# Another emission order for an attention kernel with bias: the same instructions, written in another sequence

## The chip, the cores and the metric

The kernel runs on one core of one Trainium2 chip. The metric is device time in microseconds, the median of repeated runs. Before the change it is 224.82 us (three runs, 223.55 to 225.61). The profiled execution took 223.97 us.

## The reference

Softmax attention over 4 batches times 8 heads, 1024 queries and keys, 64 channels, with one additive bias shared by all heads:

```python
scores = scale * np.matmul(q, k.transpose(0, 1, 3, 2))   # scale = 1/8
scores = scores + bias                                    # (1, 1, 1024, 1024)
attn = np.exp(scores - max) / (sum(np.exp(scores - max)) + 1e-8)
return np.matmul(attn, v)
```

q, k, v are float32 of shape (4, 8, 1024, 64). The kernel leaves the subtraction of the maximum out, since the inputs are small, and carries the bias as described below.

## The kernel before, in words

**Slots.** Each of 32 heads has 8 chunks of 128 queries, so there are 256 units of work, called slots. For each slot TensorE (PE) makes 1024 keys x 128 queries of scores in PSUM: two halves, tokens `F` and `G` (line 376, tile `pl`), each of four 128-column matmuls, or of two 256-column ones where two neighbouring chunks of a head share a round. `pl` has three double banks, so at most three slots are in flight. Only the first head of a run adds the bias with extra matmuls (line 373); the later ones carry the difference in an enlarged contraction: 64 rows hold this head's q and k, the other 64 hold the negated q and the k of the head before, and so PSUM is never cleared and each fill moves the bank from one head's scores to the next one's. A bank must have been read before it is filled again.

**Exponentials.** For 227 slots ScalarE (ACT) reads the banks and writes the exponential to `E` (line 399): tokens `X`, and `P`/`Q` where a round of three slots is read in two steps of three half banks. For 29 slots VectorE (DVE) makes it in six steps, tokens `f r s h c l` (scale to an integer in `dy`, which frees the bank, then fraction, square, shift, cube, and a last step that assembles the result in `de`).

**Output.** Token `A` multiplies a slot's exponentials with v (line 462, eight matmuls of 65 columns into `po`; the 65th column sums the row). Up to seven slots share a PSUM bank of `po`. There are two such banks, `xa` and `xb`; the letter behind an `A` opens a new one. The transposes of q and k (token `T`, lines 276 and 282, tile `px`) use the same two. `R` takes the reciprocals of a full bank and `M` multiplies and writes `ob` (both DVE), and `M` issues the stores: slots of one bank that are neighbours in head and chunk are joined into one store (line 664, SP's queue).

**Preparation of a pair of heads.** Loads go through GpSimd's (POOL's) queue: k, q at lines 213, 222 and 233, v at 246 and 250, bias at 239. `S` (DVE) sets two heads side by side, `T` transposes, `C` copies out of PSUM, `D` (DVE) makes the negated or shifted copies for the first nine pairs. From pair 9 on, `N` negates q on DVE and DMAs in SP's queue (line 603) place `ke` and `qe`. `V` (DVE) places the v rows of early pairs.

**What sets the order.** Nothing is scheduled by rules: the string `ORDER` lists 1430 tokens, and each engine gets its instructions in the order of that list. The tokens `U` and `L` each issue the next load of a fixed list; `L` also makes it wait for the DVE instruction last written before it. `SIZES` says how many slots each of 38 output banks takes. An engine runs its own list strictly in order; between engines semaphores wait for data and buffers. A load also waits for the landing of one issued four or five places before it.

```python
for token in ORDER.split():
    do(token)
...
asked.append(vec.last if kind == "L" else None)
...
flight.append(jobs.pop(0)().ins)
j = i - (BEHIND[i] if i < len(BEHIND) else 4)
```

Of the kernel before, what the change touches and what calls it, by code (L numbers as in the profile page):

```python
# [8 lines left out]
F32 = mybir.dt.float32  # L9
# [18 lines left out]
F50 G50 Tr0b r43 X50 A38 F51 Cr0 G51 F52 X51 A39 Dr0p3 Dq6p2 F53 G53 r48 A37 X53 G52 F54 R5 r32 G54 X52 Sr1 F56 s43
G56 X54 Dr0p1 F55 s32 Tr1b X56 M5 G55 F57 G57 X55 Cr1 F59 G59 h43 A42a Dr1p0 A56 X57 Dr1p1 F58 h32 G58 f59 A46 X58 A44
F60 G60 A45 c32 X60 F61 G61 s48 A47 F62 X61 A54b R6 L U r59 G62 F63 A49 L M6 X62 F64 G64 l32 A50 X64 L U U A55 G63  # L30
A53a h48 A62 X63 F65 R7 c43 G65 F67 L G67 M7 X65 A61 c48 A51 A52 F66 s59 X67 G66 F68 G68 A60 X66 f68 F70 G70 A58 A63b
X70 F69 l43 G69 F71 A57 X69 G71 F73 r68 l48 A67 X71 F72 G72 A66 G73 X72 F74 R8 h59 G74 X73 F75 f74 L G75 A65 X75 A48
F76 G76 M8 A64 X76 F77 R9 G77 s68 A73a F78 X77 G78 c59 L F79 G79 A69 l59 L U X79 A70 F80 G80 A76 X78 f80 F82 G82 A72
A75 X82 F81 M9 G81 F83 r74 G83 X81 F85 G85 f83 A43 A71b X85 F84 G84 A81 r83 X84 F86 G86 A78 Dq8p1 L U F88 X86 s74 G88
F87 G87 s83 A82 X87 A79 h74 L F89 G89 h68 L U A77 X88 A59 F90 R11 R10 c74 G90 X89 F91 M10 G91 X90 l74 F92 X91 G92 M11
A32a F93 r80 X92 G93 A87 A91 s80 F94 X93 G94 A85 h83 F95 c68 G95 X94 A92 A74 A84 F96 X95 h80 G96 A89b R12 c83 F97 M12
G97 X96 F98 c80 A90 G98 X97 A86 l68 A88 F99 G99 X98 Tq9a A94 Cq9 F100 X99 G100 A93 l80 A68 F101 X100 G101 F102 Tk9a
R13 X101 M13 G102 F103 Nq9 L G103 A96b X102 Ck9 L F104 G104 A101 f104 A97 X103 F105 G105 Tk10a X105 l83 F106 G106 F107
G107 X106 F108 f107 G108 A80 A100 X108 F109 G109 Ck10 A99 X109 F110 G110 r107 A95 F111 X110 R14 G111 M14 A98a F112
A106 r104 X111 G112 Tq10b A103 X112 Cq10 F113 G113 A109 F114 Nq10 X113 G114 s107 Tq11b F115 X114 Cq11 G115 F116 G116  # L40
h107 L A108 X115 F117 f116 L U G117 Tk12b X117 F118 G118 Ck12 A105 A102 X118 F120 R15 G120 s104 Tk11b X120 F121 M15
G121 F119 Ck11 L G119 X121 F123 G123 f119 A83a A112 X123 F124 G124 Tq12b c107 X124 F122 Cq12 G122 F126 A110 X122 l107
L G126 A114 F127 X126 G127 A113 r119 F125 A111 X127 G125 s119 Tk13b F129 h104 X125 G129 Ck13 A115 F130 G130 R16 X129
Nq11 L U A118b F128 Nq12 A124 c104 G128 X130 A117 A123 h119 L F132 r116 G132 A130 X128 A121 A120 l104 X132 F131 G131
F133 M16 L G133 X131 F135 G135 f135 L A126a X133 F134 G134 A122 X134 A127 R17 L s116 F138 G138 F136 M17 X138 G136 F137
G137 f136 Tk14b X137 F141 G141 A129 Ck14 X141 F139 G139 c119 F140 G140 Tq14b X139 h116 r135 A104 F144 X140 Cq14 L F142
G142 A125 r136 G144 X142 A128 A137b R18 L U U F143 s136 X144 G143 F145 c116 L U G145 A107 X145 A133 s135 F147 A132 M18
G147 X143 A131 F148 l116 A138 G148 X147 F146 A134 G146 R19 Tq13a X148 M19 F150 G150 h135 A141b X146 h136 F151 G151
Cq13 L U U A139 A116 X150 c136 F149 G149 A140 l119 X151 F153 Tq15a X149 F154 G154 G153 A142 Nq13 Cq15 X154 F152 Nq15
G152 A143 f152 A119 X153 F157 G157 A147a X157 c135 F156 G156 F155 G155 X156 F160 f155 G160 A145 A144 X160 F159 G159  # L50
R20 A146 Nq14 X159 F158 r155 G158 A149 F163 r152 L U U X158 F162 G163 M20 A151 G162 X163 s155 A148 F161 R21 A153b M21
X162 F166 G166 l135 A156 A150 X166 G161 Tk15a h155 L F165 X161 Ck15 G165 F169 G169 c155 A159 X165 A161 F164 G164 X169
# [652 lines left out]
```

## Time and profile before

| | |
|---|---|
| median of three runs | 224.82 us (223.55 to 225.61) |
| profiled execution | 223.97 us, its span 222.2 us |
| PE busy | 214.5 us |
| ACT busy | 211.6 us |
| DVE busy | 203.6 us |
| POOL (DMA issues) busy | 72.0 us |
| granted TensorE clock | full in all 40 slices |

Three engines are busy for over nine tenths of the span. Busy time says little here: instructions of one engine overlap, and a PE that waits between matmuls is still mostly shown busy. What is read below is start-to-start spacing, what ended an engine's idle time, and the chain of work that ended last. In a row of the timeline come the start, the time from the first start to the last end, the engine, the line, the instruction with its tiles (out<-in), the count, and in brackets idle time of the engine ahead of it with what ended it.

### The profile page before, as it was taken

Reading aid. Unit: us, or ns where it says so; the run is one execution under the profiler, and the core shown is the slowest. Engines: PE = TensorE matmul, PEld = TensorE weight load, DVE = VectorE, ACT = ScalarE, POOL = GpSimd, SP = SyncE. Lnnn points to the kernel's source line nnn. Section 1 sums busy time; section 2 is a strip of 40 time slices with the busy share of each in tenths; the row PEclk is TensorE's granted clock in tenths of the full one; section 3 lists DMA queues with packets and bytes.
Section 4 is the critical chain, followed back from the end, with each engine's and each line's share of the span. In section 5 each row is a group of like instructions: output and inputs, shape, how many; then the busy total and the mean of one; then the engine's idle time right before and its main releaser. Section 6 shows DMA issues by size and latency. Waiting matters only on the chain.

```text
span 222.2 us, 9043 instructions
## 1 busy us (share of the span) xinstructions
PE 214.5 (97%) x3965; PEld 197.5 (89%) x3965; DVE 203.6 (92%) x354; ACT 211.6 (95%) x229; POOL 72.0 (32%) x90
## 2 busy tenths in 40 slices
PE   7799999999999999999999999999999999999993
PEld 2689999999999999999998998898988999899992
DVE  2679999999999999999999999989998999999993
ACT  2799999999999999999999999999999999999992
POOL 8824446637464563030635675410000000000000
PEclk9999999999999999999999999999999999999999
DMA  6999999999999999297899999992111112011213
GB/s 174 227 205 216 227 236 146 173 168 190 128 169 164 88 119 166 62 91 176 102 227 204 215 144 190 119 194 57 44 43 33 55 45 66 7 44 44 86 46 106
DMA packets 86327, 28.87 MB, mean 130 GB/s; under 512 B 66384, under 2 KB 83024, under 8 KB 86288
## 3 DMA queue, kind: packets, MB, share of 16 engines
q0 software_dynamic: 62880, 14.06, 69.9%
q1 hardware_dynamic: 22704, 13.44, 22.6%
q10 hardware_dynamic: 704, 0.79, 1.3%
q8 instruction: 31, 0.51, 1.0%
q14 instruction: 8, 0.07, 0.1%
HBM read 29.36 MB, written 8.39 MB: 170 GB/s over the span
## 4 chain that ended last, share of the span: by engine, by line
ACT 78%; PE 17%; DMA 2%; DVE 1%; issue 0%; SPq 0%; DVEq 0%
ACT E L399 78%; PE pl L376 9%; PE po L462 4%; DMA dy<-in_k_dram 2%; PE px L276 2%; PE pl L373 1%; PE px L282 0%; DVE ob L85 0%; DVE de L85 0%; SPq L501 0%; DVE ko L85 0%; PE pl L276 0%; DVE rs L85 0%; DVEq L85 0%
## 5 line engine op out<-in xcount | busy, mean ns | idle before, releaser
L399 ACT ACTIVATE E<-pl 128x1024 bf16<-128x1024 f32 (+2 forms) x225 | 208.7, 1110 | 1.7 <-PE pl L376 1.6
L462 PE MATMUL po<-vall,E 128*128 128x65 bf16 x1816 | 86.9, 194 | 0.4 <-DVE ob L85 0.2
L462 PEld LDWEIGHTS <-E 128*128 128x128 bf16 x1816 | 77.3, 98 | 3.0 <-DVE ob L85 0.4
L376 PE MATMUL pl<-qo,ko 128*128 128x128 bf16 (+1 forms) x752 | 77.9, 239 | 0.6
L376 PE MATMUL pl<-qe,ke 128*128 128x128 bf16 (+1 forms) x648 | 67.2, 239 | 0.5 <-DVE qe L85 0.2
L376 PEld LDWEIGHTS <-ko 128*128 128x128 bf16 x856 | 57.4, 98 | 6.0 <-ACT E L399 2.1
L376 PEld LDWEIGHTS <-ke 128*128 128x128 bf16 x648 | 43.4, 98 | 5.1 <-ACT E L399 2.2
L85 DVE TENSOR_SCALAR dy<-pl 128x1024 int32<-128x1024 f32 x29 | 35.4, 1221 | 3.7 <-PE pl L376 3.4
L85 DVE SCALAR_TENSOR_TENSOR de<-dy,ds 128x1024 uint16<-128x1024 int32 x29 | 35.1, 1217 | 0.2
L213 POOL DMA_DIRECT2D q<-in_q_dram x18 | 16.6, 921 | 23.8 <-DVE de L85 8.8
L213 POOL DMA_DIRECT2D k<-in_k_dram x18 | 15.9, 887 | 24.1 <-DVE q L85 10.2
L85 DVE TENSOR_TENSOR ob<-po,rs 128x448 f32<-128x448 f32 (+3 forms) x38 | 22.7, 600 | 0.4
L250 POOL DMA_DIRECT2D vall<-in_v_dram x18 | 17.9, 996 | 11.9 <-DVE de L85 4.2
L85 DVE TENSOR_SCALAR de<-dy 128x1024 f16<-128x1024 uint16 x29 | 19.8, 695 | 0.1
L85 DVE TENSOR_TENSOR ds<-de 128x1024 f16<-128x1024 f16 x29 | 19.5, 674 | 0.2
L85 DVE TENSOR_TENSOR ds<-ds,de 128x1024 f16<-128x1024 f16 x29 | 19.5, 679 | 0.0
L373 PE MATMUL pl<-ident,braw 128*128 128x128 bf16 x136 | 14.0, 227 | 0.0
L85 DVE TENSOR_SCALAR qo<-px,sgn 128x1024 bf16<-128x1024 bf16 (+2 forms) x18 | 12.3, 684 | 0.7 <-PE px L276 0.7
L85 DVE TENSOR_SCALAR de<-de 128x1024 f16<-128x1024 f16 x29 | 12.6, 444 | 0.1
L462 PE MATMUL po<-vall,de 128*128 128x65 bf16 x232 | 12.5, 194 | 0.0
L373 PEld LDWEIGHTS <-braw 128*128 128x128 bf16 x136 | 11.8, 148 | 0.4
L85 DVE COPY ko<-px 128x1024 bf16<-128x1024 bf16 (+1 forms) x16 | 10.7, 669 | 1.0 <-PE px L282 1.0
(54 smaller groups left out, 126.0 us busy)
## 6 DMA issues: line engine op xcount, KB each, us to landing
ke<-ko SPq DMA_DIRECT2D x20, 128.0 KB, 4.7
k<-in_k_dram POOLq DMA_DIRECT2D x18, 128.0 KB, 5.3
q<-in_q_dram POOLq DMA_DIRECT2D x18, 128.0 KB, 4.8
out_dram<-ob SPq DMA_DIRECT2D x24, 96.0 KB, 2.8
vall<-in_v_dram POOLq DMA_DIRECT2D x18, 128.0 KB, 6.0
out_dram<-ob SPq DMA_DIRECT2D x30, 64.0 KB, 2.2
braw<-in_bias_dram POOLq DMA_DIRECT2D x7, 256.0 KB, 6.2
de<-in_v_dram POOLq DMA_DIRECT2D x7, 256.0 KB, 7.5
```

What stands on the lines that cost most here:

```text
L85: i = getattr(self.engine, name)(*args, **kwargs)
L213: return nc.gpsimd.dma_start(out=t[:, :, y, :], in_=(qf, kf)[x][pr][:, y].rearrange("p (c d) -> p c d", d=D))
L250: return nc.gpsimd.dma_start(out=vall[:, (2 * pr + t) % VR, :, :D], in_=vf[pr][:, t])
L276: m = nc.tensor.transpose(px[:, c, :], raws[pr, which, c0][:, c].rearrange("p t d -> p (t d)"), ident[:])
L373: m = nc.tensor.matmul(to, braw[:, c1, :].rearrange("p (kp kc) -> p kc kp", kc=NCH)[:, kc, :], ident8[:], start=i == 0 and order[0] == "b" ...
L376: m = nc.tensor.matmul(pl[:, 2 * x + b, i * P:(i + n) * P], kk[:, kc, :], qq[:, c:c + n, :].rearrange("p c q -> p (c q)"), start=i == 0 an ...
L399: read(nc.scalar.activation(E[:, e0:e0 + n].rearrange("p b x -> p (b x)"), pl[:, b0:b0 + n].rearrange("p b x -> p (b x)"), ACTF.Exp, scale ...
L462: nc.tensor.matmul(bank[b][:, banks[b].index(s), :], weights(s, kc), vall[:, slots[s][2] % VR, kc, :], start=first and kc == 0, stop=kc == ...
```

## The change

Only `ORDER` and `SIZES` change. The 1430 tokens are the same ones, but for the letters that choose between `xa` and `xb`, which of the load tokens stand where, and which `A` opens a bank. The same 29 slots go to DVE; the list of loads is the same. Which slots share an output bank changes, and with it the number of stores: 116 before, 162 now, of the same bytes. The part of a store that is contiguous in DRAM is 64, 128 or 192 floats for one row; counted as such pieces, 7,040 of 256 bytes, 6,528 of 512 and 4,224 of 768 become 17,152, 4,736 and 2,048. One pair's transpose (`Tr0`) now stands ahead of the step that sets its heads side by side (`Sr0`), so it takes ten small transposes in place of five; the step itself is still done, 38 exponentials later, and nothing reads it.

```diff
-U U U U U U U U U U U U U U U U U U U U U U U U U U U U U U U U U F3 G3 Tk1a X3 F4 Ck1 G4 F2 Tq1b X4 Dk1p0 G2 Cq1
+L F3 G3 Tk1a F4 Ck1 G4 L Dk1p0 F2 U U Tq1b X3 G2 Cq1 Dq1p0 X4 F6 Dq1p1 G6 Dk1p1 U U X2 U U Sk2 F5 U L G5 F7 Tk2a L Sq2
...
-G29 A18 F30 R2 Dk6p0 G30 X29 F31 M2 Tq6b V4 G31 X30 F32 Cq6 G32 A20a f32 X31 A21 F33 G33 Tk7b X33 F34 G34 Dq6p0 Dq6p1
+U r26 Ck6 R2 G30 F30 G31 F31 X29 A21b A17 Sq6 V4 X30 X31 F32 M2 Dk6p0 G32 A18 G33 f32 F33 X33 Tq6a F34 Cq6 G34 X34 A23
...
-SIZES = (6, 7, 7, 7, 7, 7, 6, 4, 7, 7, 7, 7, 7, 7, 7, 7, 7, 7, 7, 7, 7, 7, 7, 7, 7, 7, 7, 7, 7, 5, 7, 7, 7, 7, 7, 7,
-         7, 4)
+SIZES = (6, 7, 7, 7, 7, 7, 6, 7, 7, 7, 5, 7, 7, 7, 5, 7, 7, 7, 7, 7, 7, 7, 7, 7, 7, 7, 7, 7, 7, 7, 7, 7, 7, 7, 7, 7,
+         6, 4)
```

**First place: the start of POOL's queue.** With the semaphores each row waits for (DMASW are earlier loads, DVE is VectorE): the loads of q2, v0, k3, q3 and v1 (pairs 2, 0, 3, 3, 1), before:

```order
L233 DMA q16_130<-in_q_dram 128x2x512
L246 DMA de_132<-in_v_dram 128x2x512
L222 DMA k16_212<-in_k_dram 128x2x512
L233 DMA q16_214<-in_q_dram 128x2x512 [waits DMASW0_49]
L246 DMA de_216<-in_v_dram 128x2x512 [waits DMASW1_49]
```

and now:

```order
L233 DMA q16_130<-in_q_dram 128x2x512
L246 DMA de_132<-in_v_dram 128x2x512
L222 DMA k16_212<-in_k_dram 128x2x512 [waits DVE_49]
L233 DMA q16_249<-in_q_dram 128x2x512 [waits DMASW0_49,DVE_49]
L246 DMA de_260<-in_v_dram 128x2x512 [waits DMASW1_49]
```

The sequence of loads stays; k3 and q3 now wait for a DVE step each (k3 for the negated copy of q0, q3 for the copy of k1 out of PSUM), and what stands behind them in POOL's queue waits with them.

**Second place: DVE around bank 2 of the outputs and the opening of bank 3.** `po_724` and `po_732` are bank 2 before and now, `rs` its reciprocals and `ob` its result (`M2`). Before:

```order
L85 TENSOR_SCALAR de_866<-dy_822 128x1024
L85 RECIPROCAL rs_888<-po_724 128x7
L85 COPY ke_714<-ko_862 64x1024
L85 TENSOR_TENSOR ob_900<-po_724,rs_888 128x448
L85 COPY vall_98<-de_234 128x16x64
L85 TENSOR_SCALAR qo_924<-px_905,sgn_91 128x1024
```

and now:

```order
L85 TENSOR_SCALAR de_882<-dy_831 128x1024
L85 COPY ko_884<-px_837 128x1024
L85 RECIPROCAL rs_890<-po_732 128x7
L85 COPY side_926<-q16_332 128x2x8x64
L85 COPY vall_98<-de_350 128x16x64
L85 TENSOR_TENSOR ob_935<-po_732,rs_890 128x448
```

`M2` stands a little later in DVE's queue. On PE bank 3 was opened in `xa` (`A20a`), the bank that `M2` reads; now it is opened in `xb` (`A21b`), whose last user is the transpose of k6, and the next one in `xa` behind `M2` is the transpose `Tq6a`, three fills later.

**Third place: DVE around the slots 196, 198 and 199,** which it takes itself (rows `dy<-pl` are the steps that free a bank, in the order 196, 199, 198 both times). Before:

```order
L85 TENSOR_SCALAR dy_4074<-pl_103 128x1024
L85 TENSOR_TENSOR ob_4096<-po_3846,rs_4015 128x448
L85 RECIPROCAL rs_4106<-po_3998 128x7
L85 TENSOR_SCALAR dy_4115<-pl_103 128x1024
L85 TENSOR_SCALAR dy_4145<-pl_103 128x1024
```

and now:

```order
L85 TENSOR_TENSOR ob_4102<-po_3879,rs_4051 128x448
L85 SCALAR_TENSOR_TENSOR de_3417<-dy_3415,ds_3469 128x1024
L85 TENSOR_SCALAR dy_4132<-pl_103 128x1024
L85 TENSOR_SCALAR de_4157<-dy_4132 128x1024
L85 TENSOR_SCALAR dy_4159<-pl_103 128x1024
L85 RECIPROCAL rs_4164<-po_4001 128x7
L85 TENSOR_SCALAR dy_4172<-pl_103 128x1024
```

The last step of another slot (`l152`, the SCALAR_TENSOR_TENSOR) and the second step of slot 196 have moved ahead of the step that frees slot 199's bank. The negation of q12 (`N`) also moves on DVE: from beside that of q11 to directly ahead of that of q13, with its two copies in SP's queue directly ahead of q13's two.

More of the change, by code (lines that the diff above doesn't have):

```diff
@@ L28 @@
[L28 to L52, printed above, removed]
@@ new lines @@
+X95 A92 U G97 A94a F98 U U X96 A87 c80 G98 A93 R12 F99 c83 l80 G99 A68 X97 X98 F100 G100 A89 X99 M12 l74 X100 A97 G101
+Tq9b F101 Cq9 Nq9 G102 F102 A74 F103 X101 Tk9b R13 X102 G103 G104 X103 F104 M13 A96a F105 Ck9 G105 f104 Tk10b G106
+F106 r104 X105 G107 F107 f107 G108 F108 A80 U U X106 A95 G109 F109 F110 G110 Ck10 X108 F111 Tq10b G111 X109 F112 X110
+A109 A100 G112 s104 Cq10 X111 A98b L F113 G113 A106 Nq10 R14 l83 A99 M14 U U r107 X112 h104 G114 A103 F114 Tq11a X113
+F115 G115 G116 Cq11 X114 F116 A101 X115 U F117 G117 U Tk12a G118 F118 X117 A102 A105 Nq11 X118 F120 s107 Ck12 f116
@@ new lines @@
+X140 G142 F142 F144 X142 Cq14 A125a A128 G144 A130 r135 F143 c116 F145 G145 X144 Tq13b X145 s135 r136 s136 Cq13 l119
+G143 G147 X143 A131 F147 A141 A144 G148 A134 F148 G146 A145b F146 X147 X148 X146 G150 R19 M19 F150 A119 A138 A139 G151
+F151 l116 A142 G149 Tq15a F149 X150 X151 A116 Nq12 A137 G154 F154 Nq13 h135 F153 Cq15 R20 X149 A140a X154 F152 G153
+M20 G152 G157 F157 X153 A83 F156 G156 f152 r152 G155 F155 X157 f155 X156 F160 G160 A148 A147 F159 G159 A150 X160 X159
+Nq15 h136 s152 c135 G158 F158 A146 X158 G163 A143 F163 X163 A151b F162 A149 G162 F161 G161 X162 G166 F166 A153 A156
@@ new lines @@
+G165 A158 F165 Nq14 R21 X166 M21 X161 X165 Tk15a F169 G169 A157 r155 s155 F164 A154 X169 c136 l135 G164 G168 F168 Ck15
+f164 A159a F172 G172 X168 F167 X172 l136 r164 G167 F171 A166 X167 A165 A136 G171 R22 A163 A160 X171 F175 G175 F170
+A167 M22 G170 h155 A162b X175 F174 G174 X170 A168 c155 s164 G178 R23 A171 A172 F178 F173 X174 G173 A169 F177 G177 A161
+X178 G181 F181 M23 l155 X177 f173 F176 G176 X181 F180 G180 A170 r173 f176 G184 F184 X180 X184 h164 R24 r176 F179 c164
+G179 h152 M24 s173 A177a G183 X179 A174 A175 F183 s176 F187 h176 G187 h173 A179 F182 G182 X183 G186 X187 F186 c152
@@ new lines @@
+A229 X232 G235 X233 F235 A198 M31 f235 F236 G236 X234 A227 G237 F237 X236 r231 r235 s231 A224 F238 s235 G238 F239 X237
+A223 A173a F240 P238 G239 G240 A232 Q238 A228 F241 A226 F242 G241 P241 A234 R32 h235 A238 c235 G243 M32 G242 F243 l235
+A239 R33 c219 A203b l219 h231 A236 A237 F244 G244 A230 Q241 G245 F245 X244 F246 G246 F247 f246 X245 G247 c231 A240
+A233 F248 G248 X247 G249 F249 F250 M33 X248 A235 G250 l231 A248a X249 F251 A241 A219 r246 A244 G251 P250 G252 F252
+A245 s246 A247 Q250 A231 R34 G253 F253 X253 M34 A243b A242 F254 R35 h246 G254 G255 c246 M35 X254 A251 F255 A250 A252
@@ L78 @@
+A253 A249a l246 X255 A254 R36 A246 A255 M36 R37 M37
+"""
+SIZES = (6, 7, 7, 7, 7, 7, 6, 7, 7, 7, 5, 7, 7, 7, 5, 7, 7, 7, 7, 7, 7, 7, 7, 7, 7, 7, 7, 7, 7, 7, 7, 7, 7, 7, 7, 7,
+         6, 4)
 class Recorder:
```

60 lines of the change are left out of this document (32 added, 28 removed).

## The prediction

> **What bounds the kernel now.** First the head of the page and its chain of work that ended last.
>
> ```profile
> span 222.2 us, 9043 instructions
> PE 214.5 (97%) x3965; PEld 197.5 (89%) x3965; DVE 203.6 (92%) x354; ACT 211.6 (95%) x229; POOL 72.0 (32%) x90
> ACT 78%; PE 17%; DMA 2%; DVE 1%; issue 0%; SPq 0%; DVEq 0%
> ```
>
> Three engines are nearly full, and the chain runs over ACT for 78% of the span. So the question is how far ACT is from the fastest it can do this work. The groups of ACT by shape, then three pieces of its timeline, then the end of the chain:
>
> ```profile
> L399 ACT ACTIVATE E<-pl 128x1024 bf16<-128x1024 f32 x213 | 196.5, 1104 | 0.9 <-PE pl L376 0.9
> L399 ACT ACTIVATE E<-pl 128x1536 bf16<-128x1536 f32 x8 | 11.3, 1529 | 0.0
> L399 ACT ACTIVATE E<-pl 128x512 bf16<-128x512 f32 x4 | 2.2, 598 | 0.9 <-PE pl L376 0.8
> ...
> 8.34 1.29 ACT L399 ACTIVATE E<-pl 128x512 bf16<-128x512 f32 x2 [0.77 <-PE pl L376]
> ...
> 173.24 8.36 ACT L399 ACTIVATE E<-pl 128x1024 bf16<-128x1024 f32 x9
> ...
> 202.44 5.55 ACT L399 ACTIVATE E<-pl 128x1536 bf16<-128x1536 f32 x4
> ...
> 216.86 1.16 ACT E L399
> ...
> 218.06 0.45 PE po L462 x8
> ...
> 218.75 0.42 DVE ob L85
> ```
>
> One exponential of 1024 columns is shown for 1.10 us, but they overlap: nine in a row take 8.36 us, so they start (8.36 - 1.10) / 8 = 0.907 us apart, 0.20 less than one lasts. The long ones start (5.55 - 1.53) / 3 = 1.34 apart; for the short ones I take 0.60 - 0.20 = 0.40. At these spacings all of ACT's exponentials are 213 x 0.907 + 8 x 1.34 + 4 x 0.40 = 193.2 + 10.7 + 1.6 = 205.5 us, and with the last one's 0.2 of overhang 205.7. They ran from 8.34 to 216.86 + 1.16 = 218.02, which is 209.7. **So all stalls of ACT together are 4.0 us**, and that is all an order can win: ahead of 8.34 nothing that ORDER writes is on the chain, and behind 218.02 stand an output product, a reciprocal, an evacuation and a store in both versions. Where the 4.0 us lie, ACT's timeline tells for the larger ones:
>
> ```profile
> 12.70 1.02 ACT L399 ACTIVATE E<-pl 128x1024 bf16<-128x1024 f32 x1 [0.26 <-PE pl L376]
> ...
> 37.84 2.85 ACT L399 ACTIVATE E<-pl 128x1024 bf16<-128x1024 f32 x3 [0.29 <-PE pl L376]
> ...
> 172.30 2.88 ACT L399 ACTIVATE E<-pl 128x1024 bf16<-128x1024 f32 x3 [0.32 <-PE pl L376]
> ```
>
> Idle time costs 0.20 more than the bracket shows, because the overlap is lost too: 0.46, 0.49 and 0.52 us. Each time PE came late with a fill. The other 2.5 us are many pieces too small for a row.
>
> **What every part of PE costs.** Three pieces of the chain where PE ran without waiting:
>
> ```profile
> 23.01 0.45 PE px L276 x8
> 23.46 0.26 PE po L462 x8
> 23.72 0.45 PE pl L376 x8
> ```
>
> An output product is 0.26, a slot's fill 0.45, a transpose of a pair 0.45. An exponential with its share of all that is about 0.9 us of PE, as long as ACT needs, so PE has hardly a reserve. Added down the token list, PE's work up to each fill less ACT's 0.907 for each exponential ahead of it tells how far PE leads: from the 40th to the 120th exponential its smallest lead is 0.1 to 0.3 us larger in the new order. The amount of work is the same but for `Tr0`, five more small transposes, under 0.3 us in a place without a wait; its side copy, now unread, still costs DVE the same.
>
> **Part 1: bank 3 opens in the other PSUM bank.** DVE's timeline, then the chain across it:
>
> ```profile
> 35.54 0.18 DVE L85 RECIPROCAL rs<-po 128x7 f32<-128x7 f32 x1
> 35.65 0.43 DVE L85 COPY ke<-ko 64x1024 bf16<-64x1024 bf16 x1
> 36.01 0.60 DVE L85 TENSOR_TENSOR ob<-po,rs 128x448 f32<-128x448 f32 x1
> ...
> 36.67 0.69 PE po L462 x16
> 37.36 0.46 PE pl L376 x8
> 37.84 124.06 ACT E L399 x135
> ```
>
> The evacuation of bank 2 (36.01 to 36.61) ends and PE's product starts at 36.67, the fill behind it follows, then ACT at 37.84 with the 0.49 above. In the new order this product goes to `xb`, free since the copy of k6, and the next user of `xa` is a transpose three fills later. The wait goes. What is late next there is DVE, which gains nothing; I count -0.5, at worst 0 (another stall in its place).
>
> **Part 2: DVE's steps around slots 196, 198, 199.** DVE's and PE's timelines:
>
> ```profile
> 170.37 1.22 DVE L85 TENSOR_SCALAR dy<-pl 128x1024 int32<-128x1024 f32 x1 [0.35 <-PE pl L376]
> ...
> 171.65 0.61 PE L376 MATMUL pl<-qo,ko 128*128 128x256 bf16 x4
> ```
>
> The step that frees slot 199's bank ends at 171.59 and the fill of slot 202 starts at 171.65: this is the stall ahead of 172.30. In the new order a last step (1.13 from start to start) and a second step (0.60) stand ahead of it and a reciprocal (0.11) behind; before, DVE idled 0.35 here and some 0.5 ahead of slot 196, and that idle time takes up most of the 1.62. By these counts the step starts within 0.1 of where it did, while the fill stands 0.3 earlier in PE's list. So the stall stays and grows by about 0.3 (between -0.5, if PE's lead takes it up, and 1.62 - 0.85 = +0.8).
>
> DVE also pays for neighbours: a reciprocal starts the next instruction 35.65 - 35.54 = 0.11 later, but 218.75 - 218.53 = 0.22 where that one reads its result (a reciprocal stands at 218.53 in the chain).
>
> ```profile
> 218.53 0.19 DVE rs L85
> ```
>
> Steps that stand directly behind the one they read are 26 before and 40 now; 14 x 0.11 = 1.6 us more of DVE. Its busy time is 18 us under the span, so this lies beside other work everywhere but in part 2, whose bound holds it.
>
> **Part 3: the first loads wait for DVE.** POOL's and DVE's timelines and three DMAs with their time to landing (the first load of POOL, k3, q3):
>
> ```profile
> 7.88 0.77 POOL L222 DMA_DIRECT2D k<-in_k_dram  x1
> 8.62 0.73 POOL L233 DMA_DIRECT2D q<-in_q_dram  x1
> ...
> 9.52 0.24 DVE L85 TENSOR_SCALAR qe<-qo 64x384 bf16<-64x384 bf16 x1
> 10.77 0.69 DVE L85 COPY ko<-px 128x1024 bf16<-128x1024 bf16 x1 [1.01 <-PE px L282]
> ...
> 17.71 0.42 DVE L85 COPY side<-k 128x1024 bf16<-128x1024 bf16 x1
> ...
> braw<-in_bias_dram POOLq DMA_DIRECT2D x1, 256.0 KB, 5.2
> ...
> k<-in_k_dram POOLq DMA_DIRECT2D x1, 256.0 KB, 9.5
> q<-in_q_dram POOLq DMA_DIRECT2D x1, 256.0 KB, 10.0
> ```
>
> k3 is issued at 7.88, and its gate ends at 9.76: +1.9. q3 moves from 8.62 to 11.46: +2.85, and v1, k4, q4 behind it by the rest of that. But the same size lands in 5.2 us when it is first and in 9.5 or 10.0 here, so these transfers stand 4.3 to 4.8 us in line behind earlier ones. The delay is less than the line: landing stays at about 17.4 for k3, which DVE uses at 17.71 (and one step later in the new order). I take 0; the line is the cover, and without it the shift of 2.85 is what it costs.
>
> **Part 4: stores and the copies of q12.** DMAs of SP's queue behind the loads' end (150 us on), the copies of q13, and the first fill that needs q12:
>
> ```profile
> out_dram<-ob SPq DMA_DIRECT2D x10, 96.0 KB, 1.7
> out_dram<-ob SPq DMA_DIRECT2D x13, 32.0 KB, 1.5
> ...
> qe<-q SPq DMA_DIRECT2D x3, 128.0 KB, 5.5
> ...
> 134.70 0.41 DVE L85 TENSOR_SCALAR q<-qo 128x1024 bf16<-128x1024 bf16 x1
> ...
> 140.48 0.38 PE L376 MATMUL pl<-qe,ke 128*128 128x256 bf16 x2
> ```
>
> A store of 256-byte pieces lands in 1.5, one of 768-byte pieces in 1.7: 46 more of the small ones are 46 more issues in SP's queue, beside everything. Of what waits behind them only the copies matter. q12's negation now stands where q13's stood, near 134.7 less one step of 0.4; issued at 134.3 to 134.7, landed after 5.5, they are there at about 140, and the fill that needs them stands at 140.5 or up to 0.6 later. I take 0, with up to +1.3 if a store is in front. [...]
>
> **The sum.** Against the profiled execution's 223.97 (its span 222.2 and 1.8 around it): part 1 -0.5, part 2 +0.3, the small stalls 2.5 x about one eighth for the larger lead, -0.3, parts 3 and 4 zero: 223.5. The median of the runs, 224.82, is 0.85 above the profiled execution; half of that goes on top, as I can't tell which of the two the new runs resemble: 224.0.
>
> **The rivals.** (a) Forecast, no difference: 224.0, between 222.8 and 225.5. Chance 0.68. (b) The order removes nearly all stalls: 0.49, 0.52 and the 2.5, that is 3.5; 220.5 against the profile, 221.3 against the median. Speaking for it is the larger lead everywhere; against it, that three engines with 0.9 us of work per exponential leave no room. Halfway, with two thirds, it is 222.3. Chance 0.12. (c) The other side: the line in front of k3 and q3 is not the cover, so every early load, of which each waits for an earlier one's landing, comes 2.85 later. DVE then sets k3 aside late, PE gets its transposes late and ACT stalls before the 20th exponential: 223.5 + 2.85 = 226.4, or 227.2 with the median's 0.85. It decides from a landing of k3 later than 18.1. For it speaks that k3 landed (17.4) only 0.3 ahead of its use; against it the 4.3 us in line. Chance 0.13. (d) q12's copies come late behind stores: +1.3, 224.8 to 225.7, deciding from a landing after 141. Chance 0.07. [...]
>
> A measurement of this kernel tells about 1% from no change, 2.2 us: the runs before lie 0.9% apart. (a) gives a twentieth to each outside, (b) four fifths to faster, (c) six tenths to slower, (d) a quarter. Faster by over 1%: 0.68 x 0.05 + 0.12 x 0.8 = 0.13; slower: 0.034 + 0.078 + 0.018 = 0.13, and with what I have not seen in a list of 1430 tokens 0.15; same 0.72. The range leaves out the far ends of (b) and (c): 222.2 to 227.0.
>
> **What would show it.** Part 1: no bracketed idle time of ACT between 30 and 40 us. Part 2: an idle time of ACT of 0.3 or more near 172 us, with the step `dy` of slot 199 ending just ahead of a fill. Part 3: k3 and q3 issued near 9.8 and 11.5 and landing in about 7.5 us. Part 4: PE not waiting for `qe` near 141 us. It would be wrong if ACT's stalls, worked out as above, came to under 2 or over 6 us: then the small stalls, which I moved by one eighth, are the story.

## The result, and the profile after

The new order takes 226.56 us (median of four runs, 225.39 to 227.58) against 224.19 for the old one on the same chip: a ratio of 1.0109, interval 1.0069 to 1.0150. It is slower by 1.1%; forecast was no difference, 224.0. The profiled execution took 227.58, its span is 225.7: 3.5 us more than the span of before. First the head of its page and its chain of waits:

```profile
span 225.7 us, 9108 instructions
PE 216.7 (96%) x3970; PEld 198.6 (88%) x3970; DVE 205.9 (91%) x354; ACT 212.6 (94%) x229; POOL 70.3 (31%) x90
PE 59%; ACT 18%; DVE 14%; DMA 5%; issue 1%; SPq 0%; DVEq 0%
```

The busy times say nothing; the chain says a lot. It ran over ACT for 78% of the span and now does so for 18%, with PE at 59% and DVE at 14%. The exponentials no longer follow one another by themselves; something ahead of them decides. ACT's rows, in the same views as before (groups by shape, three pieces of the timeline), and the chain's last row:

```profile
L399 ACT ACTIVATE E<-pl 128x1024 bf16<-128x1024 f32 x213 | 197.5, 1095 | 1.2 <-PE pl L376 0.8
...
9.19 0.60 ACT L399 ACTIVATE E<-pl 128x512 bf16<-128x512 f32 x1 [1.75 <-PE pl L376]
...
29.25 11.31 ACT L399 ACTIVATE E<-pl 128x1024 bf16<-128x1024 f32 x12
...
174.60 45.71 ACT L399 ACTIVATE E<-pl 128x1024 bf16<-128x1024 f32 x46 [0.32 <-PE pl L376]
...
221.14 0.42 DVE ob L85
```

The exponentials run from 9.19 to 174.60 + 45.71 = 220.31. That splits the 3.5 us into three terms:

| | old order | new order | difference |
|---|---|---|---|
| ahead of the first exponential | 8.34 | 9.19 | +0.85 |
| first exponential to the last one's end | 209.7 | 211.1 | +1.4 |
| from there to the end of the span | 4.2 | 5.4 | +1.2 |

**The start** is PE's clock, by the spacing of its matmuls. PE's timeline of the prologue, whose instructions are the same in both orders, first before, then after:

```profile
1.21 4.17 PE L519 MATMUL pl<-E 128*128 128x512 bf16 x10 [1.21 <-DVE warm L85]
6.16 0.34 PE L276 MATMUL px<-ident,de 128*128 128x128 bf16 x3 [0.78 <-DVE de L85]
6.97 0.40 PE L276 MATMUL px<-ident,de 128*128 128x128 bf16 x4 [0.46 <-DVE de L85]
```

```profile
1.20 4.45 PE L519 MATMUL pl<-E 128*128 128x512 bf16 x10 [1.20 <-DVE warm L85]
6.06 0.50 PE L276 MATMUL px<-ident,de 128*128 128x128 bf16 x3 [0.41 <-DVE de L85]
6.84 0.61 PE L276 MATMUL px<-ident,de 128*128 128x128 bf16 x4 [0.28 <-DVE de L85]
```

Four transposes take 0.61 in place of 0.40, and in the run of 128-column matmuls behind them the starts lie 0.107 us apart until 10.2 us, where the old order's lie 0.056 apart. PE ran at about half its rate until then: the trace's record of a full granted clock begins at 10.24 us, that of the old order's at 4.97, while the mean over the whole execution is shown as 0.999. The same ten warm-up matmuls, 0.427 us apart, stand ahead in both.

**The end.** The transfers of the last 9 to 10 us by group (count, KB each, median us to landing), first before, then after; under each the last evacuations on DVE:

```profile
out_dram<-ob SPq DMA_DIRECT2D x2, 96.0 KB, 2.2
out_dram<-ob ACTq DMA_DIRECT2D x1, 192.0 KB, 2.1
out_dram<-ob SPq DMA_DIRECT2D x2, 64.0 KB, 1.6
out_dram<-ob SPq DMA_DIRECT2D x2, 32.0 KB, 2.0
out_dram<-ob ACTq DMA_DIRECT2D x2, 32.0 KB, 1.7
...
215.40 0.63 DVE L85 TENSOR_TENSOR ob<-po,rs 128x448 f32<-128x448 f32 x1
217.46 0.62 DVE L85 TENSOR_TENSOR ob<-po,rs 128x448 f32<-128x448 f32 x1
218.75 0.42 DVE L85 TENSOR_TENSOR ob<-po,rs 128x256 f32<-128x256 f32 x1
```

```profile
out_dram<-ob SPq DMA_DIRECT2D x7, 32.0 KB, 3.2
out_dram<-ob SPq DMA_DIRECT2D x3, 64.0 KB, 1.7
out_dram<-ob ACTq DMA_DIRECT2D x2, 64.0 KB, 2.1
out_dram<-ob SPq DMA_DIRECT2D x1, 128.0 KB, 2.7
out_dram<-ob SPq DMA_DIRECT2D x1, 96.0 KB, 4.0
out_dram<-ob ACTq DMA_DIRECT2D x1, 96.0 KB, 1.9
...
216.41 0.62 DVE L85 TENSOR_TENSOR ob<-po,rs 128x448 f32<-128x448 f32 x1
218.08 0.62 DVE L85 TENSOR_TENSOR ob<-po,rs 128x448 f32<-128x448 f32 x1
220.09 0.56 DVE L85 TENSOR_TENSOR ob<-po,rs 128x384 f32<-128x384 f32 x1
221.14 0.42 DVE L85 TENSOR_TENSOR ob<-po,rs 128x256 f32<-128x256 f32 x1
```

Old: three banks are evacuated in the 5.2 us up to the last evacuation's end, with eight stores (the view counts one more, of the bank ahead). New: four banks and thirteen stores (the view counts two more), and seven stores of 32 KB take 3.2 us to land in the median, where 1.5 was the old order's median behind 150 us. Both last evacuations end 1.2 us behind the last exponential; from there to the span's end it is 222.2 - 219.17 = 3.0 before and 225.7 - 221.56 = 4.1 after. That is 1.1 of the 1.2. The last store of SP's queue, first before, then after, shows where it lies:

```profile
219.20 0.33 SPq L664 DMA_DIRECT2D out_dram<-ob  x1
...
222.68 0.51 SPq L664 DMA_DIRECT2D out_dram<-ob  x1
```

In the old order it goes out 0.03 us behind the last evacuation's end (219.17), in the new one 1.1 behind it (221.56), since the stores ahead of it in the queue are still being issued, one of them for 1.21 us. It then lands in 1.7 us, where the two stores of the old order's last bank took 1.6 and 1.8. So in this execution the last store was late in its issue and not in its landing.

**The middle** shows in PE's waits. The first row is of before, the second of after (total, times, longest):

```profile
PEld L376 <- DVE dy L85: 0.2, 1, 0.2
```

```profile
PEld L376 <- DVE dy L85: 2.5, 10, 0.5
```

Ten fills now wait for the DVE step that frees their bank; one did before. (In the other profiles of the new order it is seven to nine, in two more of the old one it is one.) So three theories went to the chip: START (the clock at the start is chance, not the order), TAIL (the last banks' stores) and, for the middle, something of the order that had yet to be placed.

### The profile page after: what moved, and what is told of

Read it like the earlier page. It is cut to its first block, busy times and chain, and to the rows that moved or that the text cites. A ratio compares the mean times of both kernels' runs of the same rounds, so it can differ in the third digit from the quotient of the medians.

```text
span 225.7 us, 9108 instructions
## 1 busy us (share of the span) xinstructions
PE 216.7 (96%) x3970; PEld 198.6 (88%) x3970; DVE 205.9 (91%) x354; ACT 212.6 (94%) x229; POOL 70.3 (31%) x90
## 4 chain that ended last, share of the span: by engine, by line
PE 59%; ACT 18%; DVE 14%; DMA 5%; issue 1%; SPq 0%; DVEq 0%
PE pl L376 33%; PE po L462 19%; ACT E L399 18%; PE pl L373 3%; PE px L276 3%; DVE dy L85 3%; DVE de L85 3%; DMA out_dram<-ob 3%; DMA dy<-in_k_dram 2%; DVE qo L85 1%; DVE ob L85 1%; DVE qe L85 1%; DVE ds L85 1%; DVE ko L85 1%; DVE ke L85 1%
## 5 line engine op out<-in xcount | busy, mean ns | idle before, releaser
L399 ACT ACTIVATE E<-pl 128x1024 bf16<-128x1024 f32 (+2 forms) x225 | 209.7, 1102 | 3.2 <-PE pl L376 2.8
L376 PE MATMUL pl<-qo,ko 128*128 128x128 bf16 (+1 forms) x752 | 78.9, 239 | 1.2 <-ACT E L399 0.5
L376 PE MATMUL pl<-qe,ke 128*128 128x128 bf16 (+1 forms) x648 | 68.0, 239 | 0.6 <-DVE qe L85 0.2
L250 POOL DMA_DIRECT2D vall<-in_v_dram x18 | 16.2, 905 | 17.0 <-PE po L462 5.1
L85 DVE TENSOR_SCALAR de<-dy 128x1024 f16<-128x1024 uint16 x29 | 21.3, 741 | 0.3
L373 PE MATMUL pl<-ident,braw 128*128 128x128 bf16 x136 | 14.6, 235 | 0.0
L373 PEld LDWEIGHTS <-braw 128*128 128x128 bf16 x136 | 12.3, 150 | 0.3
```

Source lines behind the costliest of these rows:

```text
L85: i = getattr(self.engine, name)(*args, **kwargs)
L250: return nc.gpsimd.dma_start(out=vall[:, (2 * pr + t) % VR, :, :D], in_=vf[pr][:, t])
L373: m = nc.tensor.matmul(to, braw[:, c1, :].rearrange("p (kp kc) -> p kc kp", kc=NCH)[:, kc, :], ident8[:], start=i == 0 and order[0] == "b" ...
L376: m = nc.tensor.matmul(pl[:, 2 * x + b, i * P:(i + n) * P], kk[:, kc, :], qq[:, c:c + n, :].rearrange("p c q -> p (c q)"), start=i == 0 an ...
L399: read(nc.scalar.activation(E[:, e0:e0 + n].rearrange("p b x -> p (b x)"), pl[:, b0:b0 + n].rearrange("p b x -> p (b x)"), ACTF.Exp, scale ...
```

## The experiments

Ratios are to the kernel before, run beside each on the same chip; medians are of the runs named.

**The start.** The same kernel again, then both orders with idle matmuls in PE's early gaps:

```diff
             wrote(nc.tensor.matmul(pl[:, 4, :], zeros[:, :P], zeros, start=True, stop=True), 4)
+        idle((512, 256))       # matmuls of so many columns into the same bank
...
         pq = transposes(0, 0, 0, C0, "xa")
+        idle((128, 128))
```

> The changed kernel once more, unchanged. Its four times so far lie in two groups, 225.4/225.6 and 227.5/227.6, and those of the kernel before in two as well (twice 223.55; 224.8 and 225.6). Theory START: the two groups are two moments at which TensorE's clock goes up in the first 10 us (in the profile of before its 128-column matmuls are 0.056 us apart from 6.2 us on, in that of after 0.107 apart up to 10.2 us); then both groups appear again, some 1.0 to 2.0 us apart, and a profile from the lower group has its first exponential near 8.3 us instead of 9.19. Rival ORDER: the 0.85 us at the start belong to the new order; then every profile of this kernel has its first exponential near 9.2 us. Either way a ratio near 1.01 to the kernel before.

> After with idle matmuls that keep TensorE busy between 5.4 and 6.9 us (one of 512 and one of 256 columns behind the ten that are there, two of 128 behind the first three transposes); nothing reads them. START expects that the late clock goes: the upper group (227.5) vanishes, all times within about 0.8 us of 225.4, first exponential at 8.2 to 8.7 us in the profile. ORDER expects the times of after as they are, or 0.2 us more for the added matmuls.

> The kernel before with the same idle matmuls. START expects 223.3 to 224.0 in nearly all runs, so a ratio of 0.995 to 1.0 to the kernel before, whose upper runs go; what remains between this kernel and the same edit of after is then the order's own price, expected at 1.9 us (the lower groups' distance, 225.5 - 223.55). ORDER expects no change to either, and 1.9 + 0.85 us between them in the profiles.

The new order again: 227.11 (6 runs, 225.78 to 227.50), ratio 1.0122, first exponential at 9.25. With idle matmuls: 226.25 (225.77 to 227.01), 1.0097, first exponential at 8.23. The old order with them: 224.21 (12 runs, 223.50 to 225.21), 1.0009, interval 0.9992 to 1.0027. START held for the new order's start and for its upper group, which went (0.9 us off the median), though what is left lies around 226.25 and not around 225.4. It missed for the old order, whose median gained nothing (224.21, against 223.84 without them); that it starts with an early clock in most executions anyway is the author's estimate from this. Then both orders without the ten warm-up matmuls:

```diff
-        for i in range(10):
-            wrote(nc.tensor.matmul(pl[:, 4, :], zeros[:, :P], zeros, start=True, stop=True), 4)
```

> The kernel before without its ten warm-up matmuls. [...] The rival, that the late clock is a matter of the new order, expects the times of before.

> The same with the new order. START: as much later as the kernel before without warm-ups is, 227.3 to 228.3, and at least as late as the upper group of after (227.5); if the new order has less to spare behind its start than the old one, its price against the old order without warm-ups is above 2.0 us; if the start only shifts both, it is 2.0.

Old 225.13 (224.80 to 226.18), 1.0056; new 227.41 (226.37 to 229.26), 1.0161. First exponentials at 9.43 and 9.20. They are 0.9 and 1.2 us over their own kernels with idle matmuls (on other chips), a difference that these runs can't tell from none: a late clock costs the old order about as much as the new one. Nor does it belong to the new order: `after_tail_merged` below, which has the unchanged start, had its first exponential at 8.24. START's 227.3 to 228.3 for the new order came out (227.41), the rival's times of before for the old one did not (1.0056, interval 1.0033 to 1.0079). In the old order's profile the starts of the 128-column matmuls lay 0.107 us apart until 10.4 us, in the new order's only until about 9.3. **With the same start the order's price is 226.25 - 224.21 = 2.0 us**, without warm-up matmuls 2.3. Whether the unchanged new order started late in more of its runs than the old one (7 of its 10 times lie above 226.6, but so do 2 of 6 with idle matmuls), and why, is not settled; PE's instructions up to there are the same.

**Which half.** After slot 48 (261 tokens of work, 50 us) both orders have issued the same set, so they can be exchanged there, letters of banks adjusted; at 569 tokens (97 us) they differ by one token.

```diff
-ORDER = old
+ORDER = new[:261] + old[261:]      # new_to_50
+ORDER = old[:261] + new[261:]      # old_to_50
+ORDER = old[:569] + new[569:]      # old_to_97, without A101
```

> The new order up to slot 48 (the first 261 tokens of work, some 50 us: bank 3 in xb, the gated loads, the other tile positions), the old order from there on, bank letters exchanged behind the cut so that banks alternate; with the idle matmuls of the start, so it is compared with the old order with the same matmuls (224.21). At the cut both orders have issued the same work. Theory LATE: the new order costs nothing before 50 us (in the runs with an early clock the fill of slot 48 ends at 50.07 in the new order and at 50.00 and 50.34 in the old), so 223.5 to 224.3. Rival EARLY: loads under gates or bank 3's place cost, and their price shows here: 224.9 or more.

> The other half of the exchange: old order up to slot 48, new order from there on, same idle matmuls. LATE: the whole price of the order, 1.9 to 2.0 us, is here: 226.0 to 226.4, as the new order with idle matmuls (226.25). EARLY: 224.2 to 225.

> The same exchange at 97 us (569 tokens of work; A101 is the one that only the old order has done by then, so bank 14 takes 5 and bank 15 takes 6), old order before, new order behind, same idle matmuls. It splits what LATE finds behind 50 us: if the price is the last 5 us alone (stores of the last four banks) and the stretch behind 97 us, 225.4 to 226.0; the stretch from 50 to 97 us, where the new order's exponentials lose 0.8 us in the profiles (excess over their spacing 1.2 against 0.4), is then the difference to the run above, 0.5 to 0.8 us.

224.35 (1.0009), 225.94 (1.0078, interval 1.0046 to 1.0110) and 225.75 (the eleven runs up to 226.41; 1.0064, 1.0040 to 1.0087). LATE held to within 0.1 us of its two ranges: the first 50 us by themselves cost nothing, and over half of the price needs only the new order behind 97 us. The stretch from 50 to 97 us, expected at 0.5 to 0.8, came out at 0.2, less than the runs can tell. In the profiles of old_to_50 and old_to_97 the exponentials end at 217.97 as in the old order (218.0), and the last store lands 4.4 us behind them (old 3.0, new 3.9 to 4.3). So in these two executions the last banks are all of it.

**The tail.** Each of the last four banks, then of all banks, is stored by one transfer of the same bytes (the edit is shortened). These kernels write the rows to places of the output where they don't belong, so they serve for timing only.

```diff
                 stores = evac(b, closed.pop(b), whole)
+                if b >= 34:            # after_all_merged: if b >= 0, and the idle matmuls
+                    n = len(banks[b])
+                    stores = [(of[:, b % 32, :n, :], ob[:, :n])]
```

> After with the last four banks (34 to 37) stored by one transfer each, of the same bytes, whose pieces are 1536 or 1792 bytes (1024 for the last) instead of 256 to 768; they go to other places of the output than they belong, so these rows of the output are wrong or missing. Nothing else changes. Theory TAIL: the ten last SP stores of 2.0 to 4.0 us each, issued from 217.06 on, of which one waits 1.21 us to be issued, cost the 1.0 us by which the last landing lies behind the last evacuation in after (224.40 - 221.56 = 2.84) and not in before (221.00 - 219.17 = 1.83); then about 1.0 us less than the unchanged kernel in either group, and 1.8 us from the last evacuation's end to the last landing. Rival: the last bank's own store takes what it takes, since the DMA engines are held by something else (an instruction load of 16 KB at 219.35); then 0 to 0.3 us less.

> The new order with idle matmuls, and every bank stored by one transfer with pieces of 256 bytes times its outputs, at a wrong place of the output, so the output's rows are wrong or missing; 38 stores instead of 162. If the 46 stores that the change adds cost anything ahead of the last 5 us (they are on the queue with the copies of k and q, and share the DMA engines with the loads), it is below the run with the last four banks merged: 224.3 or less. If they cost nothing there, as the prediction had it, 224.6 to 225.2, all of the gain being that of the last four banks.

225.02 (12 runs, 1.0047, interval 1.0025 to 1.0068) and 224.94 (1.0032). TAIL held: the last landing is 2.98 and 2.90 us behind the last exponential in place of 3.9 to 4.3, and the last store goes out 0.04 us behind the last evacuation. Merging the stores of the other 34 banks as well gained nothing that can be told; the second kernel has the idle matmuls and the first hasn't, but with 38 stores the last exponential ends at 219.01, with 162 and the same start at 218.96. So ahead of the last banks the new order's stores cost nothing that shows. From 226.25 to 224.94 all stores together are 1.3 us of the 2.0 (1.5 by the ratios, 1.0097 and 1.0032). Then, with the right stores, VectorE's queue alone:

```diff
-A239 R33 c219 ... F250 M33 X248 A235 G250 ... A231 R34 G253 F253 X253 M34
+A239 R33 M33 c219 ... F250 X248 A235 R34 M34 G250 ... A231 G253 F253 X253
```

and the converse in the old order, `M34` from in front of `A235` to in front of `A247`.

> The new order (with the idle matmuls of the start) with two evacuations earlier in VectorE's queue and nothing else moved: bank 33's directly behind its reciprocal (some 207.9 us in place of 211.8) and bank 34's reciprocal and evacuation directly behind A235, which completes the bank (some 212.5 in place of 214.8 and 215.1). Theory TAIL: what costs is that the stores of four banks are issued within the last 5 us; with the two banks' ten stores gone by then, the last landing falls back from 4.07 to about 3.0 us behind the last exponential's end, and the time from 226.25 to about 225.2. Rival: what the new order's tail loses is the size of the pieces (256 bytes), wherever they are stored: no change, 226.0 to 226.4.

> The converse on the old order (with the idle matmuls): bank 34's evacuation moved behind two more steps of VectorE, to just ahead of A247, which opens the next bank in its place (from 212.4 to some 214.6 us); its three stores then go out with those of banks 35 to 37. TAIL expects the last landing 0.3 to 1.0 us later behind the last exponential (3.0 now), 224.5 to 225.2 in place of 224.21. The rival on piece sizes expects no change, as the same pieces are stored.

225.89 (1.0088, 1.0058 to 1.0119) and 224.42 (1.0018, 0.9995 to 1.0041). The landing moved by 0.4 of the 1.1 expected, to 3.68, and the last fourteen exponentials lost as much (0.5 us over their spacing in place of 0.1): the steps of DVE behind the moved evacuations came later. The converse moved it from 3.01 to 3.12. Both times miss their forecast ranges. With the earlier evacuations the last store goes out 0.17 us behind the last evacuation, but takes 2.2 to land, and the nine stores from 217 on took 1.7 to 2.8 each. So the last banks' stores are the cause, as the merged kernels show; what about them costs is not separated. Merging made them fewer and their pieces longer at once; moving them apart gained 0.4 of the landing, and moving them together in the old order cost next to nothing, which is what the rival on piece sizes expected there.

**Stores in the old order.** Banks 7 to 20 stored one output at a time, 163 stores, then the same with the new order's tokens for loads:

```diff
                 stores = evac(b, closed.pop(b), whole)
+                if 7 <= b < 21:
+                    stores = cut_up(b)      # one store for each output
```

> The old order, banks 7 to 20 stored one output at a time (pieces of 256 bytes): 47 stores more than its 116, all between 60 and 145 us, on the queue with the copies of k and q; nothing else changes, the last 16 banks' stores are those of before. If more stores cost nothing where they are issued, 223.9 as before. Theory SP-LOAD adds one thing: these stores are instructions of SP's, and in the traces of the new order (162 stores) an instruction load of 8 KB falls at 219.6 to 221.3 us, among the last stores, which in the old order is at 206 to 211; here too it should then move to the end, and the last landing go from 3.0 to some 3.3 to 3.7 us behind the last exponential: 224.2 to 224.7. Rival d of the prediction (copies of q late behind more stores): 225.2.

> The old order's computation and the 47 stores more of before_163, with the tokens that ask for loads where the new order has them (behind the same number of exponentials). before_163 stood for 5.5 us at X154 and X157, where the load of q had been issued at 129.94 and landed 7.3 to 8.2 us later, POOL having stood 3.9 us on a store. Theory LOADS: the earlier asks of the new order are what makes 162 stores affordable there (its q loads of that stretch are issued between 104.8 and 122.0); then most of the 7 us go, 224 to 226. Rival: the stores take the DMA engines' time, wherever the loads are asked for, and the new order escapes by where its stores lie: 229 to 231.

231.05 (1.0287) and 228.99 (1.0230). For the first all expectations were far too low; for the second LOADS missed (two of the 7 us went, not most), and its rival's 229 to 231 came out. The old order loses 7 us to 47 more stores. Two rows of the first kernel, PE's and POOL's timelines:

```profile
138.25 0.61 PE L276 MATMUL px<-ident,q 128*128 128x128 bf16 x8 [3.97 <-DMA q<-in_q_dram]
...
129.94 1.75 POOL L213 DMA_DIRECT2D q<-in_q_dram  x2 [3.88 <-DMA out_dram<-ob]
```

POOL stood 3.88 us, the load of q went out at 129.94 (at 124.34 in the old order), PE waited 3.97 us for it and ACT with PE: 5.5 us at two exponentials. The bracket names a store, but that store landed at 131.60, too late to have released the load. Up to 129.35 POOL stood at the semaphore of a copy `qe<-q` of SP's queue, issued at 121.86 and landed at 129.32. So what was late is mostly a copy of q: the four of that stretch took 6.2 to 7.5 us, where in the old order's profile (issued from 116.28 to 118.08) they took 4.6 to 6.1. With the new order's load tokens PE's wait for the load was gone and another came, in the view of waits:

```profile
PE pl L376 <- DMA qe<-q: 3.2, 1, 3.2
```

There the copies of q came late for PE itself. Why then does the new order carry 162 stores? The stores issued from 95 to 150 us, in the old order, the new one and the cut-up one:

```profile
out_dram<-ob SPq DMA_DIRECT2D x3, 192.0 KB, 5.3
out_dram<-ob SPq DMA_DIRECT2D x15, 32.0 KB, 4.6
out_dram<-ob SPq DMA_DIRECT2D x5, 96.0 KB, 4.2
out_dram<-ob SPq DMA_DIRECT2D x7, 64.0 KB, 4.3
```

```profile
out_dram<-ob SPq DMA_DIRECT2D x14, 64.0 KB, 5.2
out_dram<-ob SPq DMA_DIRECT2D x27, 32.0 KB, 4.3
out_dram<-ob SPq DMA_DIRECT2D x3, 96.0 KB, 4.5
out_dram<-ob SPq DMA_DIRECT2D x1, 128.0 KB, 4.6
```

```profile
out_dram<-ob SPq DMA_DIRECT2D x56, 32.0 KB, 3.7
```

30, 45 and 56. Of the 46 additional stores of the new order only 15 lie among the last loads and copies; 23 lie behind 150 us, where no load is left. The theory of a moved instruction load fell as well: in before_163 the load of 8 KB did move to 221.0 us, among the last stores, and the last landing stayed at 3.00.

**The middle.** Three of PE's standing gaps taken away, alone and with the earlier evacuations:

```diff
-Dk3p0 F15 Tq3b X14        Dq4p1 G20 L F20 X20 F21 G21 R1 Sk5 Tk5b     R3 G42 A27 c26 X40 M3 Tk8b
+Dk3p0 Tq3b F15 X14        Sk5 Dq4p1 G20 L F20 X20 F21 G21 R1 Tk5b     R3 G42 A27 M3 c26 X40 Tk8b
```

> The new order with the idle matmuls of the start and three tokens moved, at the three places where TensorE stands in its profiles and not in those of the old order: the transposes of q3 ahead of the fill F15 that waits for an exponential (0.34 us idle 3.0 us behind exponential X10 in all four runs looked at), the layout step of k5 one step earlier in VectorE's queue (0.27 in all four, the transposes of k5 wait for it), bank 3's evacuation ahead of step c26 (0.11 to 0.67, the transposes of k8 wait for it). Theory PE: between exponentials X12 and X132 TensorE is busy through and through and its idle time sets the stretch (0.2 to 0.6 us idle and 110.0 to 110.8 us long in the old order and the two that are old in one half, 0.9 to 1.6 and 111.5 to 111.8 in the new), so the stretch falls to 110.7 to 111.1 and the time from 226.25 to 225.5 to 225.9. Rival, the exponentials set it (as the prediction counted): the stretch stays at 111.5 and the time at 226.0 to 226.4.

> The three moves of the last kernel and the two earlier evacuations of the tail together, in the new order. If the middle and the tail are the two parts of its price and these moves take what they took each alone (0.4 us from the last landing, 0.5 to 0.8 from the middle), 225.0 to 225.4, so 0.4 to 0.7 % over the kernel before; with a price that lies elsewhere, 225.9.

226.44 (1.0095) and 226.31 (1.0097, interval 1.0062 to 1.0132): nothing gained. In the first, PE's idle time between 18 and 29 us shrank from 0.28 to 0.11 and came back behind 40 us; the stretch from the 13th to the 133rd exponential (X12 or X10 to X132 in the expectations) took 112.3 us, not 110.7 to 111.1. The two parts do not add up. The last exchange takes the new head away up to 29 us:

```diff
+ORDER = old[:124] + new[124:]      # old_to_29: 'A16' behind the cut, without 'Dk4p0'
```

> The old order for the first 124 tokens of work (29 us; A15a opens bank 3 as in the old order, A16 follows it), the new order behind, with the idle matmuls of the start. Theory DVE: VectorE's order in the first 30 us costs it 0.6 us of idle time (1.2 to 1.3 us between exponentials X12 and X24 in every run with the new head, 0.6 to 0.8 with the old one), and from X24 to X84 it is idle for only 0.1 us in each twelve exponentials, so that the late steps stop TensorE at X41 to X79; the old head gives the 0.6 us back: the exponentials X10 to X132 take 110.5 to 111.0 us in place of 111.5 to 111.8, and the time is 225.4 to 225.9 (the tail stays, last landing 4.0 to 4.4 us behind the last exponential). Rival: the stops belong to the new order's stretch from 29 to 97 us itself: 111.5 and 226.2.

Busy time of PE, PEld, DVE, ACT and POOL by stretch, in the new order with idle matmuls and then in old_to_29 (both have their first exponential at 8.22 or 8.23):

```profile
18.10:29.00 10.90, 10.62 (x217) 10.17 (x214) 9.70 (x22) 10.90 (x14) 4.38 (x7) 1.00 1.22 223
29.00:40.00 11.00, 11.00 (x235) 10.92 (x233) 10.90 (x22) 11.00 (x13) 7.93 (x8) 1.00 1.46 173
40.00:62.50 22.50, 22.12 (x434) 21.06 (x432) 22.04 (x42) 22.13 (x25) 11.13 (x15) 1.00 1.45 175
62.50:84.00 21.50, 21.38 (x412) 20.12 (x410) 21.40 (x34) 21.39 (x24) 12.86 (x15) 1.00 1.75 149
```

```profile
18.10:29.00 10.90, 10.90 (x234) 10.70 (x232) 10.21 (x24) 10.90 (x14) 4.64 (x7) 1.00 1.22 226
29.00:40.00 11.00, 10.94 (x223) 10.51 (x220) 10.35 (x19) 11.00 (x14) 6.97 (x8) 1.00 1.52 195
40.00:62.50 22.50, 22.45 (x443) 21.47 (x440) 22.04 (x42) 22.50 (x26) 12.34 (x16) 1.00 1.46 174
62.50:84.00 21.50, 21.50 (x414) 20.44 (x411) 21.30 (x36) 21.50 (x25) 13.34 (x14) 1.00 1.69 138
```

With the new head DVE does 0.5 us less up to 29 us (9.70, 10.21), then runs full (10.90 of 11.00, 21.40 of 21.50), and PE and ACT lose 0.4 us from 40 to 62.5. With the old head DVE has 0.65 us to spare from 29 to 40, PE loses 0.05 in the third row, and the stretch from the 13th to the 133rd exponential takes 110.45 us in place of 111.6 (the rival's 111.5 is out, for this execution). The time is 225.99 (1.0085, 1.0055 to 1.0115): 0.1 above its forecast range and only 0.3 below the whole new order, which is less than these runs can tell.

That DVE's lost time in the first 30 us is the source of the later waits is therefore not shown, and two other profiles speak against it. `after_early_evac` is the new order up to 207 us and has the same DVE times (9.62 up to 29 us, 10.89 of 11.00 behind), yet its stretch takes 110.8; `new_to_50` has the new head (9.59) and takes 110.7, little more than the old order's 110.6. The profiled executions also differ: that of old_to_29 (225.24) is the fastest of its seven and that of after_early_evac (225.04) of its six, that of the new order with idle matmuls (226.25) lies in the middle. What stays is that the waits of PE's weight loads for `dy` between 18 and 125 us come with the new order: none in three profiles of the old one, 0.7 to 2.1 us in those of the new. What sets them off, and the 0.5 to 0.7 us that are left beside the tail, stay open.

No kernel tried beats the old order.

## Why the prediction was wrong, point by point

**The step that failed is the bound on what can change.** The prediction said of the time behind 218.02 that there "stand an output product, a reciprocal, an evacuation and a store in both versions" and gave it no term. That term is +1.1 us in the profile, where the last store goes out 1.1 us behind the last evacuation in place of 0.03, and 1.3 to 1.5 us in the runs with merged stores, the largest part of the order's 2.0. The tokens showed it: in the new order `M34` and `M35` stand among the last three exponentials, and `M33` ahead of them has six stores to the old order's three. Part 4 counted the 46 stores as "beside everything", which held until the last banks, whose stores have nothing to lie beside.

**Ahead of 8.34** the claim was right that nothing of ORDER counts, but the 0.85 us of clock there were not foreseen; they come and go with the execution and cost the two orders 0.9 and 1.2 us when the warm-up is left out. They are a part of the distance between runs that the prediction took for scatter of the measurement, but not all: the old order with idle matmuls still spreads from 223.50 to 225.21.

**Part 1** held where it was looked for: ACT's row from 29.25 has no bracket up to 40 us, and the 0.49 is gone. Its value did not: the new order's fill of slot 48 ends at 50.07 and the old one's at 50.00 and 50.34 in two profiles, and new_to_50 gained nothing (224.35 against 224.21). "What is late next there is DVE" was named and then counted as -0.5 all the same; from 29 to 40 us DVE is busy for 10.90 of 11.00.

**Part 2.** The stall stayed, with the step of slot 199 ending just ahead of the fill, as foreseen. These are the rows of DVE's and PE's timelines:

```profile
172.67 1.23 DVE L85 TENSOR_SCALAR dy<-pl 128x1024 int32<-128x1024 f32 x1
...
173.95 0.61 PE L376 MATMUL pl<-qo,ko 128*128 128x256 bf16 x4
```

It did not grow: 0.32 in the bracket of 174.60, as before. The +0.3 was 0. Its working was loose as well: the idle times of 0.35 and 0.5 make 0.85, about half of the 1.62 and not most of it, so by these counts the step was not placed within 0.1.

**The neighbours on DVE** were put "beside other work everywhere but in part 2", by a busy time 18 us under the span. That is the second error: an average over the whole span. Between 29 and 84 us of the new order's profile DVE has 0.05 to 0.2 us to spare in 11. Whether the neighbours cost anything there is not shown; most of the additional ones lie behind 92 us.

**The small stalls** were to shrink by 0.3 for a larger lead of PE, counted against ACT's spacing. They grew: all stalls of ACT come to 211.1 - 205.7 = 5.4 us in place of 4.0, of which some 0.3 lie in the late start and most of the rest between 19 and 131 us. The two orders overlap in this, though: after_early_evac comes to 4.5 and the old order with idle matmuls to 5.2. A lead of PE counted by tokens is not one if its fills wait for `dy`.

**Part 3** held. k3 went out at 10.45 and q3 at 12.92, later than the 9.8 and 11.5 by the late clock, and landed in 6.4 and 5.2 us, at 16.9 and 18.1: the line in front of them was the cover. Rival (c) is out, and new_to_50, which has these gates, confirms it. **Part 4's copies** held too: PE did not wait for `qe` near 141. Yet rival (d)'s mechanism is real, as before_163_newloads shows with 3.2 us; the new order keeps clear of it, most likely by where its stores are.

**The chances.** Two sums are off by a tenth (223.5 + 0.43 is 223.9, 14 x 0.11 is 1.5), which changes nothing. The rivals searched the head of the program and the copies; none was at the end. Slower by over 1% had 0.15, and the range's upper end of 227.0 did hold the median, for a reason that the prediction did not have.

## What to carry to other kernels

Here the last transfers had nothing behind them, and 1.3 of the 2.0 us lay there: when an order, a grouping or a bank layout changes, list what is evacuated and stored in the last few microseconds, how many stores that makes and when each goes out behind the others of its queue, and give this a term of its own. Look for spare time of an engine stretch by stretch, never by its share of the span: here DVE, with 18 us to spare in 222 before, had 0.1 in eleven of them in the new order, and PE's weight loads waited ten times for its steps `dy`, 2.5 us in all. Before a profile of one kernel is set against that of another, see whether both executions lie alike among their kernels' runs: the stretch read here differed by 1 us between executions with the same order in it. And count with more than one price for more transfers: 47 more cost one order 7 us among loads and copies, while the other order's 46, mostly elsewhere, cost nothing that shows ahead of its last banks; that what shares their queue and time sets the price is the author's reading of these two.

## What the runs showed of the hardware beyond that

A packet of a store took 18 ns for 256 bytes, 27 for 512 and 36 for 768 (medians in both orders): between these sizes 9 ns more for each 256 bytes more.

Instruction loads of 16 KB, one every 4 to 10 us, took 0.9 to 1.9 us each in the old order's trace (the trace doesn't say for which engine they are). Single executions show PE standing 0.5 to 0.6 us with nothing to wait for ("issue"), at places that change from run to run: the profiled run of the old order with idle matmuls, its slowest (225.21), has such stops near 45 and 51 us. Whether the loads cause the stops was not tried.
